# A decoder trunk: eight of the 22 row chunks of each down projection in seven products instead of eight

## The chip, the cores and the metric

One core of one Trainium2 chip runs the whole program. The metric is the device time in microseconds; several runs of each kernel are compared by their median.

## The reference

Two layers, each of three sublayers; x is 512 tokens by 1024 columns in float32, and the hidden width of the feed-forward is 2816.

```python
def swiglu_ffn(x, w_gu, w_down):
    a, u = jnp.split(x @ w_gu, 2, axis=-1)
    return (jax.nn.silu(a) * u) @ w_down

for l in range(DEPTH):                       # DEPTH = 2
    x = layer_norm(ALPHA * x + 0.5 * swiglu_ffn(x, ffn1_w_gu[l], ffn1_w_down[l]), ...)
    x = layer_norm(ALPHA * x + hybrid_mixer(x, w_in[l], w_out[l], ...), ...)
    x = layer_norm(ALPHA * x + 0.5 * swiglu_ffn(x, ffn2_w_gu[l], ffn2_w_down[l]), ...)
```

So there are four feed-forwards. Their down projection, h (512 x 2816) times w_down (2816 x 1024), is what the change concerns.

## The kernel before

**Three passes.** Every large product is made from operands cut in two float32r parts: `split` (L158) casts the high part on ScalarE (L159) and subtracts it from the source on VectorE (L160). `mm3` (L165) then multiplies high by high, high by low, low by high, three matmuls into one PSUM bank (L168, L169, L170).

**Weights.** `Weights` walks one list of items for the whole program. An item names a raw tile of 1 MB (two buffers, loaded on the queue of SyncE), and how to cut a *unit* from it: high and low part, each 128 x 1024, six buffers (`UBUFS`). `pump` cuts units up to `LOOK` = 6 ahead of their use; `done` gives buffers back and pumps. An item whose raw is None loads nothing.

**A feed-forward** (`ffn`, L434) has a gate/up stage and a down stage. The gate/up stage takes 11 pairs of 128 hidden rows. Nine of them (`SEVEN`) are already made in the seven-product form (`glu7`): `seven_items` (L276) forms sums of weight blocks on VectorE in tiles S (two buffers), and `sums_of_x` those of x in Th and Tl. The hidden values go to `hT`, 128 x 22 x 512. Before the last pair, the activations of the first two chunks are split ahead into a unit taken from the weights' pool (`early`, L568).

**The down stage** (L582) has all eight PSUM banks as `acc[t][q]`: four tiles of 128 tokens by two halves of 512 columns. For each of the first 18 chunks of 128 hidden rows it splits a chunk of `hT` two chunks ahead (`halves`; pool buffers hh and hl, four each), takes a weight unit of 128 rows x 1024 columns, and does `mm3` for each t and q: 24 matmuls of 128 x 128 by 128 x 512. The last four chunks (`TAIL`) are held in buffers of their own and done tile by tile, so that `norm` (L404) of a tile can run beside the next tile's matmuls. `norm` adds ALPHA times Y, the residual kept in SBUF, to the banks (L411), and does the layer norm on VectorE with one power on GpSimd (L419). Its scale and shift are loaded in chunk 7 (`load_ln`, L400).

**Order.** A framework sets the order of each engine's instructions when the program is built, by program order among those it holds to be ready, and places the semaphores. Tiles of one tag share their buffers in turn.

Of the kernel before, what the change touches and what calls it, by code (L numbers as in the profile page):

```python
# [7 lines left out]
F32 = mybir.dt.float32  # L8
F32R = mybir.dt.float32r
AF = mybir.ActivationFunctionType  # L10
ALU = mybir.AluOpType
# [17 lines left out]
TAIL = 4  # L29
# [3 lines left out]
DELAY = (4, 3, 9, 9)  # L33
# [59 lines left out]
class Trunk:  # L93
# [182 lines left out]
    def seven_items(self, a, u):  # L276


        sums = {}

        def blocks(v):
            h = KC // 2
            return v[:, :h, :P], v[:, h:, :P], v[:, :h, P:], v[:, h:, P:]

        def wide(t):
            return t.rearrange("p (k c) -> p k c", k=KC)

        def first(v, hi, lo):
            hv, lv = wide(hi), wide(lo)
            self.split(hv, lv, v[:, :, :P])  # L290
            return hv, lv

        def s12(q):
            def go(v, hi, lo):
                s = sums[q] = self.gpool.tile([P, 4, KC // 2, P], F32, tag="S", name=self.nm("S"), bufs=2)
                a11, a12, a21, a22 = blocks(v)
                self.nc.vector.tensor_add(s[:, 0], a21, a22)
# [25 lines left out]

    def ffn_items(self, gu, down, key):
        items = []
        for fp in range(NFP):
            a = self.cols_item(gu, fp * 256, (key, "a", fp))
            u = self.cols_item(gu, DFF + fp * 256, (key, "u", fp))
            if fp == 0:
                items += [a[0], u[0], a[1], u[1]]  # L330
            else:
                items += self.seven_items(a, u) if fp in SEVEN else a + u
        for fp in range(NFP):
            late = [self.tail_units if fp * 2 + c >= NF - TAIL else None for c in range(2)]
            items += self.rows_item(down, fp * 256, (key, "d", fp), late)
        return items

    def mix_items(self, w_in, w_out, key):
        items = self.cols_item(w_in, KA, (key, "kv"))
# [55 lines left out]
        self.to_xT(self.Y[:, t, 512:], t, 4)  # L395
        yield 0

    def load_ln(self, pool, g, b, tag="ln"):
        gb = pool.tile([P, 2, D], F32, tag=tag, name=self.nm("ln"))
        self.nc.sync.dma_start(gb[:, 0, :], g.partition_broadcast(P))  # L400
        self.nc.sync.dma_start(gb[:, 1, :], b.partition_broadcast(P))
        return gb[:, 0, :], gb[:, 1, :]

    def norm(self, t, halves, gb, out=None, delay=4):  # L404
        nc = self.nc
        g, b = gb
        y = self.Y[:, t, :]
        st = self.small.tile([P, 2, 6], F32, tag="st", name=self.nm("st"))
        for h in range(2):
            hs = slice(h * 512, (h + 1) * 512)  # L410
            nc.vector.scalar_tensor_tensor(out=y[:, hs], in0=y[:, hs], scalar=ALPHA, in1=halves[h],  # L411
                                           op0=ALU.mult, op1=ALU.add)
# [4 lines left out]
        nc.vector.tensor_scalar_add(ve, mv[:, 1:2], LN_EPS)  # L417
        rs = self.small.tile([P, 1], F32, tag="rs", name=self.nm("rs"))
        nc.gpsimd.tensor_tensor(out=rs, in0=ve, in1=self.mhalf[:, 0:1], op=ALU.pow)  # L419
# [11 lines left out]
    def tail_units(self):  # L431
        return self.units(self.fpool, "tl", TAIL)

    def ffn(self, g, b, out=None):  # L434
        nc, tc, W = self.nc, self.tc, self.W
        with ExitStack() as ctx:
            hpool = ctx.enter_context(tc.tile_pool(name=self.nm("ffnh"), bufs=1))
            gctx = ExitStack()
            gp = self.gpool = gctx.enter_context(tc.tile_pool(name=self.nm("ffng"), bufs=1))
            hT = hpool.tile([P, NF, SEQ], F32, name=self.nm("hT"))  # L440
# [94 lines left out]
            for fp in range(NFP):  # L535
                if fp == 0:
# [4 lines left out]
                    more = []  # L541
# [13 lines left out]
                if fp == 1:  # L555
                    a1, u0 = us[5], W.get()
                    for i in range(2):
                        t0 = i * 256
                        u = self.ps()
# [6 lines left out]
                    continue  # L566
                if fp == NFP - 1:
                    early = W.take()  # L568
                    hv = [v.rearrange("p (f t) -> p f t", f=2) for v in early]
                    self.split(hv[0], hv[1], hT[:, 0:2, :])  # L570
                if fp in SEVEN:
                    self.finish([xs])
                    glu7(fp)
# [12 lines left out]
            def halves():  # L586
                for f in range(2):
                    yield hv[0][:, f, :], hv[1][:, f, :]
                for f in range(2, NF):
                    hh = pool.tile([P, 512], F32R, tag="hh", name=self.nm("hh"), bufs=TAIL)  # L590
                    hl = pool.tile([P, 512], F32R, tag="hl", name=self.nm("hl"), bufs=TAIL)
                    self.split(hh, hl, hT[:, f, :])
                    yield hh, hl

            def down(f, u, h, t, q):
                ts = slice(t * P, (t + 1) * P)
                hs = slice(q * 512, (q + 1) * 512)
                self.mm3(acc[t][q], (h[0][:, ts], h[1][:, ts]), (u[0][:, hs], u[1][:, hs]), f == 0, f == NF - 1)

            split = halves()  # L600
            ahead = [next(split), next(split)]
            for f in range(NF - TAIL):
                if f == NF // 3:
                    gb = self.load_ln(pool, g, b)
                u, h = W.get(), ahead.pop(0)
                ahead.append(next(split))
                for t in range(NT):
                    for q in range(2):
                        down(f, u, h, t, q)
                    if t % 2:  # L610
                        self.step()
                W.done(2 if f == 1 else 1)
# [396 lines left out]
```

## Time and profile before

| | |
|---|---|
| median of 3 runs | 1847.43 us (1847.25 to 1847.91) |
| the profiled execution | 1847.67 us |
| its span in the profile | 1845.9 us |
| TensorE matmuls | 1831.1 us busy, 12170 instructions |
| VectorE | 1262.3 us busy |
| ScalarE | 841.9 us busy |
| GpSimd | 84.9 us busy |
| DMA | 184.89 MB, mean 100 GB/s |

PE is TensorE, PEld its weight loads, DVE is VectorE, ACT ScalarE, POOL GpSimd, SP SyncE; SPq is the queue from which SyncE issues transfers. A row of a group reads: line, engine, operation, output <- inputs, shapes, count | busy us, mean ns of one | idle us of the engine before them, and what ended it. A row of the order in time reads: start us, us, engine, line, operation, names, shapes, count [idle before, and what ended it]. A row of transfers reads: output <- input, queue, count, size of one, median us from issue to landing. A busy PE is not PE at its peak, since matmuls overlap.

### The profile page before, as it was taken

The numbers are of one execution on the slowest core, as the hardware profiler recorded it, in microseconds if no ns is written. First come the engines' busy times: TensorE is split into PE (matmuls) and PEld (weight loads), VectorE is DVE, ScalarE is ACT, GpSimd is POOL, SyncE is SP. The second block draws the span as 40 slices with busy tenths as digits, with TensorE's granted clock in tenths as the row PEclk, the third lists the DMA queues.
The fourth block names the chain that finished last, engine by engine and source line by source line (L and its number), as shares of the span: only waits on it lengthen the run. The fifth ranks groups of instructions, "written<-read, shape, count | busy, mean of one in ns | idle before, by whom it ended". The sixth has DMA issues, their size and how long they took to land.

```text
span 1845.9 us, 29148 instructions
## 1 busy us (share of the span) xinstructions
PE 1831.1 (99%) x12170; PEld 1669.2 (90%) x12170; DVE 1262.3 (68%) x1830; ACT 841.9 (46%) x1391; POOL 84.9 (5%) x72
## 2 busy tenths in 40 slices
PE   9999999999999999999999999999999999999998
PEld 9999988897789999988899999888877899999886
DVE  7788744656758788853687887447567687887435
ACT  4455533178723455543234555332786234555330
POOL 0000000111110000000000000001111100000001
PEclk9999999999999999999999999999999999999999
DMA  5233244122122322333312323341233122342321
GB/s 183 92 115 114 92 143 152 63 83 88 50 92 69 115 92 92 125 135 121 100 61 97 95 92 115 137 143 58 81 92 92 46 92 92 97 133 92 137 92 46
DMA packets 136948, 184.89 MB, mean 100 GB/s; under 512 B 3952, under 2 KB 115312, under 8 KB 136816
## 3 DMA queue, kind: packets, MB, share of 16 engines
q1 hardware_dynamic: 136816, 183.03, 30.4%
q8 instruction: 95, 1.56, 0.4%
q14 instruction: 37, 0.30, 0.1%
HBM read 180.92 MB, written 2.10 MB: 99 GB/s over the span
## 4 chain that ended last, share of the span: by engine, by line
PE 87%; issue 6%; DVE 3%; ACT 2%; DMA 1%; POOL 1%; SPq 0%; POOLq 0%; DVEq 0%; ACTq 0%
PE ps L168 28%; PE ps L169 28%; PE ps L170 28%; PE ps L388 1%; POOL sw L780 1%; DMA raw<-in_ffn_w_gu_dram 1%; ACT sw L778 1%; PE ps L888 0%; ACT b L820 0%; DMA retS<-c_retS_dram 0%; ACT uh L159 0%; DVE rr L853 0%; DVE Y L423 0%; DVE b L160 0%; PE ps L884 0%
## 5 line engine op out<-in xcount | busy, mean ns | idle before, releaser
L168 PE MATMUL ps<-xh,uh 128*128 128x256 f32 (+1 forms) x1616 | 482.8, 299 | 0.5 <-ACT uh L159 0.5
L169 PE MATMUL ps<-xl,uh 128*128 128x256 f32 (+1 forms) x1616 | 479.9, 297 | 0.3 <-DVE xl L160 0.3
L170 PE MATMUL ps<-xh,ul 128*128 128x256 f32 (+1 forms) x1616 | 479.7, 297 | 0.4 <-DVE ul L160 0.2
L160 DVE TENSOR_TENSOR ul<-raw,uh 128x1024 fp32r<-128x1024 f32 (+1 forms) x333 | 346.6, 1054 | 112.6 <-ACT uh L159 112.2
L159 ACT CAST uh<-raw 128x1024 fp32r<-128x1024 f32 (+1 forms) x333 | 299.1, 915 | 256.1 <-PE ps L169 172.3
L168 PE MATMUL ps<-Th,uh 128*128 128x256 f32 x1152 | 326.0, 283 | 0.0
L169 PE MATMUL ps<-Tl,uh 128*128 128x256 f32 x1152 | 326.0, 283 | 0.0
L170 PE MATMUL ps<-Th,ul 128*128 128x256 f32 x1152 | 326.0, 283 | 0.0
L168 PEld LDWEIGHTS ps<-xh,uh 128*128 128x128 f32 x1616 | 309.3, 191 | 10.8 <-issue 1.6
L170 PEld LDWEIGHTS ps<-xh,ul 128*128 128x128 f32 x1616 | 309.1, 191 | 9.2 <-DVE ul L160 0.8
L169 PEld LDWEIGHTS ps<-xl,uh 128*128 128x128 f32 x1616 | 309.3, 191 | 8.4 <-DVE xl L160 0.8
L168 PE MATMUL ps<-uh,hh 128*128 128x512 f32 x640 | 249.5, 390 | 0.0
L170 PE MATMUL ps<-uh,hl 128*128 128x512 f32 x640 | 249.0, 389 | 0.0
L169 PE MATMUL ps<-ul,hh 128*128 128x512 f32 x640 | 249.0, 389 | 0.0
L160 DVE TENSOR_TENSOR ul<-S,uh 128x1024 fp32r<-128x1024 f32 x144 | 175.9, 1222 | 73.5 <-ACT uh L159 72.9
L159 ACT CAST uh<-S 128x1024 fp32r<-128x1024 f32 x144 | 151.0, 1048 | 160.5 <-PE ps L169 159.2
L168 PEld LDWEIGHTS ps<-Th,uh 128*128 128x128 f32 x1152 | 221.2, 192 | 0.0
L169 PEld LDWEIGHTS ps<-Tl,uh 128*128 128x128 f32 x1152 | 221.2, 192 | 0.0
L170 PEld LDWEIGHTS ps<-Th,ul 128*128 128x128 f32 x1152 | 221.2, 192 | 0.0
L160 DVE TENSOR_TENSOR hl<-hT,hh 128x512 fp32r<-128x512 f32 x80 | 54.2, 690 | 173.4 <-ACT hh L159 173.4
L159 ACT CAST hh<-hT 128x512 fp32r<-128x512 f32 x80 | 48.6, 622 | 207.4 <-PE ps L169 206.2
L170 PEld LDWEIGHTS ps<-uh,hl 128*128 128x128 f32 x640 | 120.1, 188 | 25.0
(131 smaller groups left out, 2256.0 us busy)
## 6 DMA issues: line engine op xcount, KB each, us to landing
raw<-in_ffn_w_gu_dram SPq DMA_DIRECT2D x86, 1024.0 KB, 5.4
raw<-in_ffn_w_down_dram SPq DMA_DIRECT2D x44, 1024.0 KB, 4.9
raw<-in_w_in_dram SPq DMA_DIRECT2D x18, 1024.0 KB, 5.3
raw<-in_w_in_dram SPq DMA_DIRECT2D x8, 512.0 KB, 4.7
raw<-in_w_out_dram SPq DMA_DIRECT2D x8, 512.0 KB, 6.5
raw<-in_w_out_dram SPq DMA_DIRECT2D x4, 1024.0 KB, 4.9
ln<-in_ln_g_dram SPq DMA_DIRECT2D x6, 512.0 KB, 5.2
ln<-in_ln_b_dram SPq DMA_DIRECT2D x6, 512.0 KB, 6.5
```

The lines of the kernel that those rows point to most:

```text
L159: a = self.nc.scalar.copy(hi, src)
L160: b = self.nc.vector.tensor_sub(lo, src, hi.bitcast(F32))
L168: mm(out, ah, bh, start=start, stop=False, **kw)
L169: mm(out, ah, bl, start=False, stop=False, **kw)
L170: mm(out, al, bh, start=False, stop=stop, **kw)
L388: nc.tensor.transpose(b[:, c * P : (c + 1) * P], src[:, c * P : (c + 1) * P], self.ident)
L778: nc.scalar.copy(sw[q * 32 : q * 32 + 32, :n], src[o * 32 : o * 32 + 32, :n])
L780: nc.gpsimd.tensor_mul(sw[:, :n], sw[:, :n], S)
```

## The change

The first eight chunks, 1024 hidden rows, are taken as a product of 2 x 2 blocks: the activations in blocks of 256 tokens by 512 hidden rows, the weights in blocks of 512 hidden rows by 512 columns. Seven products of blocks take the place of eight. Each product has two steps (g = 0, 1) of 256 hidden rows, and a step has 12 matmuls on one weight unit (256 rows x 512 columns) and one activation pair.

- Weights: W11, W21 and W22 come as raw tiles (`wide_item`). Sums of blocks stand in two tiles R (tag S, now in a pool that lives as long as the feed-forward): W11 and W12 are loaded to them, and the other blocks are added by transfers with an adding operation, issued on GpSimd's queue. `cut` splits a unit from R and issues the next adds behind it.
- Activations: sums of blocks are formed in place in `hT` on VectorE (`fifth`, `third`).
- Products that belong to several blocks of the output are added up in the PSUM banks; where a bank holds a sum that another block needs, `into` puts it into Y with one VectorE operation, and the bank goes on.
- Chunk 8 stands between product 6 and product 7; chunks 9 to 21 are as before. `norm` scales Y by ALPHA only where `into` has not done so.
- The split ahead holds the operand of product 1 (256 tokens of four chunks). Scale and shift are loaded in chunk 12, in a buffer of R's tag.

```diff
-        for fp in range(NFP):
+        for fp in range(4, NFP):
...
+        return items + self.down_items(down, key, R, rows[0]) + rows[1:]
+
+    def down_items(self, w, key, R, row):
+        def block(i, j, g):
+            r0 = i * 512 + g * 256
+            return w[r0 : r0 + 256, j * 512 : (j + 1) * 512].rearrange("(k p) c -> p k c", p=P)
+        def add(g, x, i, j):
+            self.nc.gpsimd.dma_start(R[g][:, x], block(i, j, g), accum_op=ALU.add)
+        def begin(go):
+            def f(v, hi, lo):
+                for g in range(2):
+                    R[g] = self.spool.tile([P, 2, 2, 512], F32, tag="S", name=self.nm("R"), bufs=2)
+                    for x in range(2):
+                        self.nc.sync.dma_start(R[g][:, x], block(0, x, g))
+                    add(g, 0, 0, 1)
+                return go(v, hi, lo)
+            return f
+        def cut(g, x, *after):
+            def go(v, hi, lo):
+                hv, lv = (t.rearrange("p (k c) -> p k c", k=2) for t in (hi, lo))
+                self.split(hv, lv, R[g][:, x])
+                for a in after:
+                    add(g, *a)
+                return hv, lv
+            return (None, None, None, go)
+        p1, p2, p3 = (self.wide_item(w, j * 512, i, (key, "b", i, j)) for i, j in ((0, 0), (1, 0), (1, 1)))
+        p1[0] = p1[0][:3] + (begin(p1[0][3]),)
+        return (p1 + p2 + [cut(g, 0, (0, 1, 1), (1, 1, 1)) for g in range(2)]
+                + [cut(g, 0, (0, 1, 0)) for g in range(2)] + p3 + [cut(g, 1) for g in range(2)]
+                + [row] + [cut(g, 0) for g in range(2)])
...
+            def part(g, i, j):
+                return hT[:, j * 4 + 2 * g : j * 4 + 2 * g + 2, i * 256 : (i + 1) * 256]
+            def fifth(g):
+                a11, a21, a22 = part(g, 0, 0), part(g, 1, 0), part(g, 1, 1)
+                hh, hl = (v.rearrange("p (f t) -> p f t", f=2) for v in pair())
+                s1 = self.s1[:, g]
+                nc.vector.tensor_sub(s1, a21, a22)
+                nc.vector.tensor_sub(a21, a11, a21)
+                nc.vector.tensor_sub(a11, s1, a11)
+                self.split(hh, hl, s1)
+                return hh, hl
+            def third(g):
+                nc.vector.tensor_add(part(g, 0, 1), part(g, 0, 1), part(g, 0, 0))
+                return operand(part(g, 0, 1))
...
+            def seventh(banks, u, h, new):
+                for f in range(2):
+                    for i, b_ in enumerate(banks):
+                        ts = slice(i * P, (i + 1) * P)
+                        self.mm3(b_, (h[0][:, f, ts], h[1][:, f, ts]), (u[0][:, f, :], u[1][:, f, :]),
+                                 new and f == 0, False, skip_group_check=True)
+                self.step()
...
+            def into(banks, t0, q, scale, sign=ALU.add):
+                for i, b_ in enumerate(banks):
+                    y = self.Y[:, t0 + i, q * 512 : (q + 1) * 512]
+                    nc.vector.scalar_tensor_tensor(out=y, in0=y, scalar=scale, in1=b_, op0=ALU.mult, op1=sign)
+            for n, (banks, new, more) in enumerate((
+                    (low, True, (0, 0, ALPHA)), (left, True, None), (high, True, (0, 1, ALPHA)),
+                    (low, False, (0, 1, 1.0, ALU.subtract)), (right, True, None),
+                    (low, False, (2, 1, ALPHA, ALU.subtract)), (low, False, None))):
+                if n == 6:
+                    chunk(8)
+                for g in range(2):
+                    u, h = W.get(), ahead.pop(0)
+                    ahead.append(next(split))
+                    seventh(banks, u, h, new and g == 0)
+                    W.done(2 if n == 0 and g == 1 else 1)
+                if more:
+                    into(banks, *more)
+            for f in range(9, NF - TAIL):
+                if f == 12:
+                    gb = self.load_ln(self.spool, g_, b, "S", 2)
+                chunk(f)
...
-                self.norm(t, acc[t], gb, out, DELAY[t])
+                self.norm(t, acc[t], gb, out, DELAY[t], (1.0 if t < 2 else ALPHA, 1.0))
```

Here `low` and `high` are the banks of tokens 256 to 511, columns 0 to 511 and 512 to 1023, and `left` and `right` those of tokens 0 to 255. `ahead` holds activation pairs three steps ahead of their use, and `chunk` does the 24 matmuls of a chunk as before, the two banks of `low` last.

More of the change, by code (lines that the diff above doesn't have):

```diff
@@ L294, in go @@
             def go(v, hi, lo):
-                s = sums[q] = self.gpool.tile([P, 4, KC // 2, P], F32, tag="S", name=self.nm("S"), bufs=2)
+                s = sums[q] = self.spool.tile([P, 4, KC // 2, P], F32, tag="S", name=self.nm("S"), bufs=2)
                 a11, a12, a21, a22 = blocks(v)
@@ L402, in load_ln, with norm @@
         return gb[:, 0, :], gb[:, 1, :]
-    def norm(self, t, halves, gb, out=None, delay=4):
+    def norm(self, t, halves, gb, out=None, delay=4, scale=(ALPHA, ALPHA)):
         nc = self.nc
@@ L432, in tail_units, with ffn @@
         return self.units(self.fpool, "tl", TAIL)
-    def ffn(self, g, b, out=None):
+    def ffn(self, g_, b, out=None):
         nc, tc, W = self.nc, self.tc, self.W
@@ L584, in ffn, with pair @@
             acc = [[self.ps() for _ in range(2)] for _ in range(NT)]
-            def halves():
-                for f in range(2):
[L588 to L593, printed above, removed]
+            def pair():
+                return [pool.tile([P, 512], F32R, tag=tag, name=self.nm(tag), bufs=TAIL) for tag in ("hh", "hl")]
@@ new lines, in part, with operand @@
+            def part(g, i, j):
+                return hT[:, j * 4 + 2 * g : j * 4 + 2 * g + 2, i * 256 : (i + 1) * 256]
+            def operand(src):
+                hh, hl = (v.rearrange("p (f t) -> p f t", f=2) for v in pair())
+                self.split(hh, hl, src)
+                return hh, hl
+            self.s1 = pool.tile([P, 2, 2, 256], F32, tag="tlh", name=self.nm("s1"), bufs=TAIL)
+            def fifth(g):
+                a11, a21, a22 = part(g, 0, 0), part(g, 1, 0), part(g, 1, 1)
+                hh, hl = (v.rearrange("p (f t) -> p f t", f=2) for v in pair())
+                s1 = self.s1[:, g]
[3 more added lines that the diff above has]
+                self.split(hh, hl, s1)
+                return hh, hl
@@ new lines, in third, with whole, operands @@
+            def third(g):
+                nc.vector.tensor_add(part(g, 0, 1), part(g, 0, 1), part(g, 0, 0))
+                return operand(part(g, 0, 1))
+            def whole(f):
+                hh, hl = pair()
+                self.split(hh, hl, hT[:, f, :])
+                return hh, hl
+            def operands():
+                for g in range(2):
+                    yield operand(part(g, 0, 1))
+                for g in range(2):
+                    yield fifth(g)
+                for g in range(2):
+                    yield operand(part(g, 0, 0))
+                for g in range(2):
+                    yield third(g)
+                for g in range(2):
+                    yield operand(part(g, 1, 0))
+                yield whole(8)
+                for g in range(2):
+                    yield operand(part(g, 1, 1))
+                for f in range(9, NF):
+                    yield whole(f)
@@ L597, in down @@
                 hs = slice(q * 512, (q + 1) * 512)
[L598 to L604, printed above, removed]
+                self.mm3(acc[t][q], (h[0][:, ts], h[1][:, ts]), (u[0][:, hs], u[1][:, hs]), False, f == NF - 1,
+                         skip_group_check=True)
@@ L605, in ffn, with chunk @@
+            split = operands()
+            ahead = [(hv[0][:, g], hv[1][:, g]) for g in range(2)] + [next(split)]
+            def chunk(f):
                 u, h = W.get(), ahead.pop(0)
                 ahead.append(next(split))
[L607 to L610, printed above, removed]
+                for i, (t, q) in enumerate(((0, 0), (0, 1), (1, 0), (1, 1), (2, 1), (3, 1), (2, 0), (3, 0))):
+                    down(f, u, h, t, q)
+                    if i % 4 == 3:
@@ new lines, in ffn @@
+            for n, (banks, new, more) in enumerate((
[4 more added lines that the diff above has]
+                    chunk(8)
+                for g in range(2):
+                    u, h = W.get(), ahead.pop(0)
[4 more added lines that the diff above has]
+                    into(banks, *more)
```

21 lines of the change are left out of this document (13 added, 8 removed).

## The prediction

> **What bounds the kernel now.** I read the page's busy time and chain first, then the busy time in stretches, then the groups by shape, then the order of work around one down projection.
>
> ```profile
> PE 1831.1 (99%) x12170; PEld 1669.2 (90%) x12170; DVE 1262.3 (68%) x1830; ACT 841.9 (46%) x1391; POOL 84.9 (5%) x72
> ...
> PE 87%; issue 6%; DVE 3%; ACT 2%; DMA 1%; POOL 1%; SPq 0%; POOLq 0%; DVEq 0%; ACTq 0%
> ```
>
> TensorE is busy 1831.1 of 1845.9 us and the chain lies on it for 87%. The stretches are the 18 chunks of the first down projection (its last four come behind them), some gate/up work, and the first 5.5 us of the same projection.
>
> ```profile
> core 0: us, PE busy (x) PEld busy (x) DVE busy (x) ACT busy (x) POOL busy (x), PEclk, DMA share, GB/s
> 239.00:337.10 98.10, 98.10 (x435) 81.26 (x434) 41.05 (x43) 33.96 (x43) 0.00 (x0) 1.00 0.43 140
> 571.50:670.00 98.50, 98.50 (x768) 96.02 (x767) 84.41 (x116) 44.44 (x65) 3.04 (x2) 1.00 0.34 108
> 239.00:244.50 5.50, 5.50 (x27) 4.54 (x26) 4.06 (x6) 3.13 (x5) 0.00 (x0) 1.00 0.90 309
> ```
>
> In the down projection TensorE has no gap and the granted clock is 1.00, while VectorE works 41.05 of 98.10 us. So a matmul taken out there is worth its whole spacing, as long as what replaces it stays under the cover. The gate/up row shows how far cover reaches: VectorE busy 84.41 of 98.50 us and TensorE still without a gap.
>
> ```profile
> L168 PE MATMUL ps<-uh,hh 128*128 128x512 f32 x640 | 249.5, 390 | 0.0
> L168 PE MATMUL ps<-uh,uh 128*128 128x512 f32 x64 | 24.9, 390 | 0.0
> ```
>
> The order in time, TensorE and then VectorE:
>
> ```profile
> 238.89 0.28 PE L170 MATMUL ps<-Th,ul 128*128 128x256 f32 x1
> 239.01 0.40 PE L168 MATMUL ps<-uh,uh 128*128 128x512 f32 x1
> ...
> 294.06 0.69 DVE L160 TENSOR_TENSOR hl<-hT,hh 128x512 fp32r<-128x512 f32 x1 [3.27 <-ACT hh L159]
> ...
> 337.58 0.69 DVE L160 TENSOR_TENSOR hl<-hT,hh 128x512 fp32r<-128x512 f32 x1 [3.27 <-ACT hh L159]
> ```
>
> The two groups before are one of the three passes of all down matmuls: 704 over four projections, 176 each, 8 for each of 22 chunks. Their 390 ns overlap, so the price is the spacing: the activation split comes once a chunk, and from 294.06 to 337.58 lie 8 chunks, 5.44 us each, 24 matmuls of 226.7 ns.
>
> **The change: matmuls.** Eight chunks cost 8 x 24 = 192 matmuls. The form with seven products costs 7 x 2 steps x 12 = 168, with the same operand shapes. Per projection 24 go, 5.44 us; over four, 96, 21.76 us. A step of 12 takes 2.72 us; I count time T from the projection's first matmul (239.01), so step k starts at 2.72 k, products 1 to 6 fill steps 0 to 11, chunk 8 runs from 32.6 to 38.1, and product 7 follows.
>
> [...]
>
> **The change: VectorE and ScalarE.** Prices from the groups, then the order in time at the start of a projection:
>
> ```profile
> L160 DVE TENSOR_TENSOR ul<-raw,uh 128x1024 fp32r<-128x1024 f32 x227 | 276.2, 1221 | 95.7 <-ACT uh L159 95.4
> L159 ACT CAST uh<-raw 128x1024 fp32r<-128x1024 f32 x227 | 237.0, 1049 | 190.6 <-PE ps L169 110.9 <-DMA raw<-in_ffn_w_gu_dram 32.7 <-PE ps L170 20.9
> L160 DVE TENSOR_TENSOR hl<-hT,hh 128x512 fp32r<-128x512 f32 x80 | 54.2, 690 | 173.4 <-ACT hh L159 173.4
> L159 ACT CAST hh<-hT 128x512 fp32r<-128x512 f32 x80 | 48.6, 622 | 207.4 <-PE ps L169 206.2 <-DVE ul L160 1.3
> L297 DVE TENSOR_TENSOR S<-raw 128x512 f32<-128x512 f32 x72 | 49.5, 688 | 1.4 <-DMA raw<-in_ffn_w_gu_dram 0.3
> L411 DVE SCALAR_TENSOR_TENSOR Y<-Y,ps 128x512 f32<-128x512 f32 x48 | 32.7, 683 | 25.8 <-PE ps L170 25.4
> ```
>
> ```profile
> 239.28 0.42 DVE L521 SCALAR_TENSOR_TENSOR hT<-ps,s 128x256 f32<-128x256 f32 x1 [0.59 <-PE ps L170]
> 240.17 1.23 DVE L160 TENSOR_TENSOR ul<-raw,uh 128x1024 fp32r<-128x1024 f32 x1 [0.46 <-ACT uh L159]
> 241.31 2.49 DVE L160 TENSOR_TENSOR hl<-hT,hh 128x512 fp32r<-128x512 f32 x4
> 250.97 2.36 DVE L160 TENSOR_TENSOR ul<-raw,uh 128x1024 fp32r<-128x1024 f32 x2 [3.99 <-ACT uh L159]
> 240.04 2.18 ACT L159 CAST hh<-hT 128x512 fp32r<-128x512 f32 x4
> 244.67 1.05 ACT L159 CAST uh<-raw 128x1024 fp32r<-128x1024 f32 x1 [2.45 <-PE ps L170]
> ```
>
> Per projection come six more weight splits (14 for 8), six more activation splits (14 for 8), six subtractions for product 3, two additions for product 5, and eight updates of Y from the banks (rows of L411's kind). VectorE: 6 x 1.22 + 6 x 0.69 + 8 x 0.69 + 8 x 0.68 = 22.4 us. ScalarE: 6 x 1.05 + 6 x 0.62 = 10.0 us. ScalarE needs 1.67 us in a step of 2.72 and is no limit.
>
> VectorE is tight. Its strictest date is the start of product 6 (step 10, T = 27.2), which needs the update of Y after product 4 because it adds into the same banks. Due by then, from T = 0.7 when the gate work's last piece (239.28) ends: 7 weight splits, 9 activation splits, 8 sums, 6 updates. At single durations 8.5 + 6.2 + 5.5 + 4.1 = 24.3 of 26.5 us; at the rates of the runs of four and two (0.62 and 1.18 us apart) 22.5. Laying the pieces one behind another, each no earlier than its buffer is free, I get no TensorE wait at the second rate and 1.67 us at the first (in steps 9 and 10). Four projections: 0 to 6.7 us. The queued work of this kernel shows the second rate, so I take a sixth, 1.1 us.
>
> Each update of Y waits for TensorE to end its product; behind it on VectorE stand later splits. The order is not the program's: the casts of four activation chunks run at 240.04, ahead of the weight cast that the program has second and that runs at 244.67. So a piece that is known to wait lets ready ones pass. Within the other dates: the first activation split that is not done ahead (product 2, T = 5.4) ended at about 242, T = 3; the split done ahead covers only product 1, 5.4 us where it was 10.9.
>
> **The change: loads, adds, queues.**
>
> ```profile
> q1 hardware_dynamic: 136816, 183.03, 30.4%
> raw<-in_ffn_w_down_dram SPq DMA_DIRECT2D x44, 1024.0 KB, 4.9
> raw<-in_w_in_dram SPq DMA_DIRECT2D x8, 512.0 KB, 4.7
> raw<-in_ffn_w_gu_dram SPq DMA_DIRECT2D x3, 512.0 KB, 7.6
> ```
>
> ```profile
> 225.82 1.23 DVE L160 TENSOR_TENSOR ul<-S,uh 128x1024 fp32r<-128x1024 f32 x1 [0.52 <-ACT uh L159]
> 232.78 6.30 SPq L265 DMA_DIRECT2D raw<-in_ffn_w_down_dram  x2
> 239.73 0.34 SPq L400 DMA_DIRECT2D ln<-in_ln_g_dram  x1
> 240.12 0.42 SPq L401 DMA_DIRECT2D ln<-in_ln_b_dram  x1
> 344.53 1.52 POOL L419 TENSOR_TENSOR rs<-ve,mhalf 128x1 f32<-128x1 f32 x1 [343.23 <-DVE ve L417]
> ```
>
> SP loses one load of 1 MB per projection (10 for 11) and gets four of 512 KB into the sum tiles. They wait for the last reading of the gate work's S tiles (225.82 to 227.05, T = -12); what stands behind them, the load at 232.78, comes later than four issues of 0.4 us, so nothing is held. At 309 GB/s the 2 MB are in by about T = -4; a first add to each half follows, due before the split at T = 0 and at the latest 2.3 us before step 4, T = 8.6. Two adds of 3.1 us meet both. The scale and shift loads move from chunk 7 to 12; they land within 8 us and are due 30 us later. Both cost nothing; their cover is the six units of lookahead.
>
> POOL issues eight adds of 512 KB per projection; it has no other work there (idle 343.23 us until 344.53). No row shows an adding transfer. Lower end: the plain load, 1.5 us of all engines (0.90 share gave 309 GB/s) and 4.7 us to landing. An add has twice to read, so 3.1 us apart and 7.6 us to landing is my middle; the upper end is one after another at 7.6 us each. The binding chain: the split of product 3's weights (steps 4, 5) reads the sums, then POOL adds two blocks for each half, and product 4's second half (step 7, T = 19.0) needs its split, 2.3 us, so the third add must have landed by 16.8. First adds are released at about 2.4, the third at 5.9. Middle: max(5.9, 2.4 + 6.2) + 7.6 = 16.2, no wait. At the plain end it lands at 10.6. At c us each in series it lands at 2.4 + 3c: a wait beyond c = 4.8, and 8.4 us per projection at 7.6. I take 0, since with the transfers at 43% share in this stretch adds overlap as plain loads do. None of it can be a gain: TensorE has no gap here that could close.
>
> **Sum.** The profiled execution took 1847.67 us, 0.24 over the median of 1847.43. 1847.67 - 21.76 + 1.1 = 1827.0.
>
> **Rivals.**
> - VectorE is the bound in the products, or adds of 4.8 to 6.3 us in series hold product 4. For it: only 2 us are spare at T = 27.2. Against: the gate/up row with VectorE at 84.41 of 98.50 and no gap. Time: 1832.6 with VectorE's whole 6.7 us; up to 1843.9 with the adds at 6.3 us (4.5 us each projection).
> - Slower: the adds run in series at more than 6.9 us each. The wait lies before step 6 or 7 of each projection; it eats 5.44 us at c = 6.6 and more beyond. At c = 7.6, 1847.67 - 21.76 + 33.6 = 1859.5. For it: nothing in the trace bounds an add from above. Against: a plain 512 KB needs 1.5 us of the engines.
>  [...]
> - No change: c near 6.6 us, gain and wait equal, 1847.7.
>
> **How the numbers follow.** Full gain 0.63 (1824.5 to 1830), part of it held back 0.20 (1830 to 1843.9), no change 0.04, slower 0.13. About 0.2% (3.7 us) is what a measurement of this kernel can tell from no change. Faster is 0.63 + 0.20 = 0.83. The low end is 1825.9 less 1.4 for run and clock differences; the range to 1841 takes in the full gain and most of the second case and leaves out about 0.2.
>
> **What would show it.** Right: one pass of the down matmuls counts 672 for 704; each projection starts and ends 5.44 us nearer; VectorE at 1262 + 90, ScalarE at 842 + 40; TensorE without a gap in the first 44 us of a projection; adds landing under 8 us. Wrong: rows of matmuls of the products that waited on the split of the sum tile, whose cast waited for a transfer (the adds), or on a split whose VectorE piece began late (the crowd), or on an update of Y; or a spacing in the products that isn't 226.7 ns.

## The result and the profile after

The changed kernel takes 1903.28 us (1901.65 to 1903.95), the kernel before, beside it, 1847.53 us: a ratio of 1.030, 95% interval 1.0282 to 1.0318. The forecast was 1827.0 us. One run of one later kernel, the one with six sums on VectorE, took 2981.46 us at a granted clock of 0.555, against 0.999 in its other three, and is left out below.

The page of the changed kernel, its busy times, the engines' shares of the chain and the group of the adds:

```profile
PE 1823.9 (96%) x12074; PEld 1657.7 (87%) x12074; DVE 1341.5 (71%) x1942; ACT 879.6 (46%) x1439; POOL 124.3 (7%) x104
...
PE 77%; issue 10%; DVE 5%; DMA 3%; ACT 2%; POOL 2%; SPq 0%; POOLq 0%; DVEq 0%; ACTq 0%
...
R<-in_ffn_w_down_dram POOLq DMA_DIRECT2D x32, 512.0 KB, 6.0
```

TensorE has 96 matmuls fewer (12074 for 12170), as the change says. Its share fell from 99% to 96%: in a span of 1902.2 us it is not busy for 78.3 us, where it was 14.8. The adds land in 6.0 us, under the 7.6 that the forecast took for one add. So a single add is no slower than thought. The waits show what is wrong:

```profile
PE ps L168 <- ACT hh L159: 56.4, 4, 14.3
PE ps L170 <- DVE hl L160: 5.5, 8, 1.3
```

One long wait in each of the four projections, on the cast of an *activation*, an operand that needs no add. In the first projection (its first matmul starts at 239.45), TensorE's waits and then ScalarE's order in time:

```profile
252.30 0.50 PE L170 MATMUL ps<-uh,hl 128*128 128x512 f32 x1 [1.33 <-DVE hl L160]
269.14 0.80 PE L168 MATMUL ps<-uh,hh 128*128 128x512 f32 x1 [14.29 <-ACT hh L159]
```

```profile
239.53 1.05 ACT L159 CAST uh<-R 128x1024 fp32r<-128x1024 f32 x1 [0.93 <-PE ps L169]
...
248.74 1.05 ACT L159 CAST uh<-R 128x1024 fp32r<-128x1024 f32 x1 [6.59 <-DMA R<-in_ffn_w_down_dram]
261.26 1.04 ACT L159 CAST uh<-R 128x1024 fp32r<-128x1024 f32 x1 [11.48 <-DMA R<-in_ffn_w_down_dram]
267.53 1.04 ACT L159 CAST uh<-R 128x1024 fp32r<-128x1024 f32 x1 [5.22 <-DMA R<-in_ffn_w_down_dram]
268.48 0.61 ACT L159 CAST hh<-s 128x512 fp32r<-128x512 f32 x1
```

The four casts from R are the weights of product 3 (steps 4 and 5) and product 4 (steps 6 and 7). The last three waited for adds. The cast of 268.48 is the activation of step 5; it came behind both weight casts of product 4, before which ScalarE stood idle for 11.48 and 5.22 us. VectorE has the same order. The second row is the difference that this cast reads, the first the weight split of product 4 ahead of it:

```profile
262.34 1.22 DVE L160 TENSOR_TENSOR ul<-R,uh 128x1024 fp32r<-128x1024 f32 x1 [9.50 <-ACT uh L159]
...
264.08 0.68 DVE L645 TENSOR_TENSOR s<-hT 128x512 f32<-128x512 f32 x1
```

So an operand that needs no add was held on two engines by splits that wait for adds. Ahead of ScalarE's last weight cast, and with VectorE's order as it is, it could have come at 264.8, some 3.7 us earlier (an estimate from these rows). GpSimd's adds in the same projection:

```profile
226.13 1.35 POOL L349 DMA_DIRECT2D R<-in_ffn_w_down_dram  x1 [224.82 <-DVE Q L530]
232.47 1.23 POOL L349 DMA_DIRECT2D R<-in_ffn_w_down_dram  x1 [4.99 <-issue]
242.62 1.21 POOL L349 DMA_DIRECT2D R<-in_ffn_w_down_dram  x1 [8.91 <-DVE hl L160]
248.98 1.23 POOL L349 DMA_DIRECT2D R<-in_ffn_w_down_dram  x1 [5.15 <-issue]
255.22 1.21 POOL L349 DMA_DIRECT2D R<-in_ffn_w_down_dram  x1 [5.01 <-issue]
261.50 1.22 POOL L349 DMA_DIRECT2D R<-in_ffn_w_down_dram  x1 [5.07 <-DMA R<-in_ffn_w_down_dram]
267.77 1.21 POOL L349 DMA_DIRECT2D R<-in_ffn_w_down_dram  x1 [5.04 <-DMA R<-in_ffn_w_down_dram]
273.66 1.22 POOL L349 DMA_DIRECT2D R<-in_ffn_w_down_dram  x1 [4.68 <-DVE hl L160]
```

Six of them follow the one before at 5.9 to 6.4 us, about when that one has landed. The third comes 10.15 us behind the second, which took 9.9 us to land, beside a plain load of 1 MB issued at 233.22. In the order of the built program the second and the fourth of them are W22 for product 6, which has until T = 27. The adds that product 4 needs come fifth (255.22) and sixth (261.50). The sixth is landed at 267.5, and the cast starts at 267.53.

The last part is the clock. A table by stretch, the column behind POOL being the granted clock:

```profile
255.00:260.00 5.00, 0.00 (x0) 0.00 (x0) 0.00 (x0) 0.00 (x0) 1.21 (x1) 0.95 0.62 92
260.00:265.00 5.00, 0.00 (x0) 0.00 (x0) 2.66 (x4) 1.04 (x1) 1.22 (x1) 0.50 0.34 45
265.00:270.00 5.00, 0.85 (x2) 0.50 (x2) 1.76 (x3) 2.47 (x4) 1.21 (x1) 0.50 0.47 79
270.00:275.00 5.00, 4.28 (x10) 3.14 (x10) 5.00 (x7) 3.59 (x6) 1.22 (x1) 0.50 0.59 98
275.00:280.00 5.00, 5.00 (x20) 3.98 (x19) 4.87 (x7) 2.03 (x3) 0.00 (x0) 0.85 0.88 198
```

During the wait the clock falls to 0.50 and stays there for some 7 us after the matmuls go on. So a wait is paid twice.

### The profile page after: what moved, and what is told of

Same layout as the page of the kernel before. It is cut to its first block, busy times and chain, and to the rows that moved or that the text cites. A ratio compares the mean times of both kernels' runs of the same rounds, so it can differ in the third digit from the quotient of the medians.

```text
span 1902.2 us, 29290 instructions
## 1 busy us (share of the span) xinstructions
PE 1823.9 (96%) x12074; PEld 1657.7 (87%) x12074; DVE 1341.5 (71%) x1942; ACT 879.6 (46%) x1439; POOL 124.3 (7%) x104
## 3 DMA queue, kind: packets, MB, share of 16 engines
q1 hardware_dynamic: 143152, 187.23, 30.4%
## 4 chain that ended last, share of the span: by engine, by line
PE 77%; issue 10%; DVE 5%; DMA 3%; ACT 2%; POOL 2%; SPq 0%; POOLq 0%; DVEq 0%; ACTq 0%
PE ps L170 25%; PE ps L169 25%; PE ps L168 25%; DMA R<-in_ffn_w_down_dram 1%; ACT sw L896 1%; POOL sw L898 1%; DMA raw<-in_ffn_w_gu_dram 1%; POOL R L349 1%; PE ps L426 1%; DVE Y L462 1%; DVE st L452 1%; DVE ul L160 1%; ACT uh L159 1%; DVE Y L459 1%; DVE Y L450 0%
## 5 line engine op out<-in xcount | busy, mean ns | idle before, releaser
L159 ACT CAST uh<-raw 128x1024 fp32r<-128x1024 f32 (+1 forms) x325 | 291.1, 912 | 229.7 <-PE ps L169 149.3
L160 DVE TENSOR_TENSOR ul<-raw,uh 128x1024 fp32r<-128x1024 f32 (+1 forms) x325 | 336.7, 1049 | 83.5 <-ACT uh L159 83.0
L168 PE MATMUL ps<-uh,hh 128*128 128x512 f32 x640 | 254.5, 398 | 56.4 <-ACT hh L159 56.4
L170 PE MATMUL ps<-uh,hl 128*128 128x512 f32 x640 | 254.1, 397 | 5.5 <-DVE hl L160 5.5
L169 PE MATMUL ps<-ul,hh 128*128 128x512 f32 x640 | 253.1, 395 | 0.0
L168 PEld LDWEIGHTS ps<-uh,hh 128*128 128x128 f32 x640 | 122.9, 192 | 83.3 <-ACT hh L159 58.1
L169 PEld LDWEIGHTS ps<-ul,hh 128*128 128x128 f32 x640 | 122.7, 192 | 25.6
```

Source lines behind the costliest of these rows:

```text
L159: a = self.nc.scalar.copy(hi, src)
L160: b = self.nc.vector.tensor_sub(lo, src, hi.bitcast(F32))
L168: mm(out, ah, bh, start=start, stop=False, **kw)
L169: mm(out, ah, bl, start=False, stop=False, **kw)
L170: mm(out, al, bh, start=False, stop=stop, **kw)
```

## The experiments

Theory A, after this reading: only one add is under way at a time, since the room that the program reserves for GpSimd's transfers (`dynamic_dma_scratch_size`) holds no second one. With the runs it grew: the order on GpSimd, ScalarE and VectorE, and the clock behind a wait, came to it. What it and its rivals mean for a run is said in each expectation. Ratios are against the kernel before, in runs on the same chip.

**Room for two adds.** The program sets this room, here 1024 bytes.

```diff
-    nc = _bacc.Bacc("TRN2", target_bir_lowering=False, num_devices=1, dynamic_dma_scratch_size=1024)
+    nc = _bacc.Bacc("TRN2", target_bir_lowering=False, num_devices=1, dynamic_dma_scratch_size=1920)
```

> Only the space reserved per partition for the descriptors of GpSimd's transfers grows, from 1024 to 1920 bytes. Theory A (the space holds one add of 512 KB, so that an add is issued only when the one before has landed, 6.2 us apart): adds overlap, are issued about 1.2 us apart where nothing else holds them and land about 3.3 us apart; TensorE's wait of 14.3 us in each projection goes; time 1826 to 1832. Theory B (GpSimd or its queue takes one adding transfer at a time whatever the space): adds stay 6.2 us apart, time 1900 to 1906. Theory C (VectorE is the bound in the products and the adds matter little): some waits stay, on late VectorE pieces, time 1833 to 1890.

Measured: 1856.14 us, ratio 1.0047 (1.003 to 1.0064). 47 of the 56 us are gone, but the number expected was missed. GpSimd's adds, and TensorE's waits:

```profile
225.31 1.35 POOL L349 DMA_DIRECT2D R<-in_ffn_w_down_dram  x1 [224.00 <-DVE Q L530]
227.40 1.21 POOL L349 DMA_DIRECT2D R<-in_ffn_w_down_dram  x1 [0.74 <-DMA R<-in_ffn_w_down_dram]
...
241.51 1.21 POOL L349 DMA_DIRECT2D R<-in_ffn_w_down_dram  x1 [4.23 <-DVE ul L160]
246.02 1.20 POOL L349 DMA_DIRECT2D R<-in_ffn_w_down_dram  x1 [3.30 <-DVE ul L160]
```

```profile
PE ps L168 <- ACT hh L159: 11.9, 4, 3.2
PE ps L170 <- DVE hl L160: 5.2, 4, 1.5
```

The second add now starts 2.1 us behind the first, and product 4's adds at 241.51 and 246.02, not 255.22 and 261.50. They wait for VectorE's split, as the program wants. What is left is 17.1 us of listed waits, all on the activation of step 5, 11.9 of them on its cast, and TensorE busy for 1821.6 us where 1808.8 would do (below). In the first projection ScalarE's cast (254.89) now follows close on the difference that it reads; that one VectorE formed only at 254.17, behind the weight split of 252.43, whose cast waited for an add. So the room is one cause and not the only one. The time lies in theory C's range too; the run without adds (below) speaks against C, since VectorE has the same work there and no wait in the products.

**The same bytes in smaller adds.** Room as in the changed kernel, each add as two of 256 KB.

```diff
-            self.nc.gpsimd.dma_start(R[g][:, x], block(i, j, g), accum_op=ALU.add)
+            for k in range(2):
+                self.nc.gpsimd.dma_start(R[g][:, x, k], block(i, j, g)[:, k], accum_op=ALU.add)
```

> Each add of 512 KB is issued as two of 256 KB, in the space of 1024 bytes. Theory A: two or three of the small adds are in flight at a time, so an add's two halves together take less than 6.2 us, and the time falls below 1880. Theory B: each half is waited for by itself, about 3 us of fixed time and 1.6 us of transfer, 9 us for an add; time above 1930.

Measured: 1861.72 us in a single run, below 1880, as theory A has it. The halves overlap: three of them start within 2.85 us from 225.90, and a half lands 5.7 us after issue in the median. So in this run neither the queue nor the adding operation kept transfers apart. At 1024 bytes three halves were thus under way together, and the fourth started at 230.30; at 1920 bytes a second whole add started 2.1 us behind the first (above).

**The order of the adds alone.** Those for product 6 are tied behind those for products 3 and 4 and, as the pairs in the edit stand, each also behind product 7's add of its half; room as in the changed kernel.

```diff
+            if self.adds:
+                self.tc.add_manual_dep(a.ins, self.adds[-1].ins.name, NOSYNC, reason="add order")
...
-        return (p1 + p2 + [cut(g, 0, (0, 1, 1), (1, 1, 1)) for g in range(2)]
-                + [cut(g, 0, (0, 1, 0)) for g in range(2)] + p3 + [cut(g, 1) for g in range(2)]
+        return (p1 + p2 + [cut(g, 0, (0, 1, 1)) for g in range(2)]
+                + [cut(g, 0, (0, 1, 0), (1, 1, 1)) for g in range(2)] + p3 + [cut(g, 1) for g in range(2)]
```

> The two adds for product 6 in each projection, which the order of the changed kernel puts second and fourth on GpSimd's queue, go behind the adds for product 4 and later; nothing else changes, and adds stay one at a time. Theory A: the third add of the queue, which product 4 waits for, is issued at about T = 3.5 where it was the fifth at T = 16; product 4's weights are split 10 us earlier; what is left is about 4 us a projection for the activation cast that stands behind the last of these casts on ScalarE; time 1840 to 1855. Theory B the same. Theory C (VectorE): the wait shrinks by less than half, time above 1870.

Measured: 1931.39 us, ratio 1.0456 (1.044 to 1.0471). Worse than the changed kernel, the opposite of what was expected. TensorE's waits in the first projection:

```profile
257.63 0.79 PE L168 MATMUL ps<-uh,hh 128*128 128x512 f32 x1 [5.15 <-ACT hh L159]
...
274.51 0.50 PE L170 MATMUL ps<-uh,hl 128*128 128x512 f32 x1 [3.78 <-DVE hl L160]
289.08 0.80 PE L168 MATMUL ps<-uh,hh 128*128 128x512 f32 x1 [10.81 <-ACT hh L159]
```

The first wait shrank from 14.29 to 5.15, but two new ones came behind it, at steps 8 and 9. These steps are product 5, whose activation pieces stand on VectorE behind the weight splits of product 6 (272.63 and 285.30), and product 6's casts start at 271.56 and 284.23, as its adds land, now the sixth and the eighth. Eight adds 6.25 us apart are 50 us, and the products last 43.5 us, but the first two adds were issued before the products began (225.29 and 233.27). In fifth and sixth place product 6's adds would have landed near 262 and 271 (an estimate from this run's landings), with product 7's behind them. That order was not run. So this run shows its own order to be worse, and not that no order of single adds would do.

**No adds at all.**

```diff
-            self.nc.gpsimd.dma_start(R[g][:, x], block(i, j, g), accum_op=ALU.add)
+            pass
```

> All adds are left out, so the weight sums of products 3, 4, 6 and 7 are not formed; matmuls, splits, loads and updates of Y stay. Theories A and B: TensorE has no gap in the products, time 1825 to 1829, the saving of the 96 matmuls in full. Theory C: waits on VectorE stay, 0.4 us to 1.7 us a projection or more, time 1828 to 1840.

Measured: 1825.85 us, ratio 0.9884 (0.987 to 0.9899). Its page, and a table of the first 11 us of the first projection:

```profile
PE 1808.8 (99%) x12074; PEld 1650.9 (91%) x12074; DVE 1339.3 (73%) x1942; ACT 881.1 (48%) x1439; POOL 84.8 (5%) x72
```

```profile
239.00:250.00 11.00, 11.00 (x50) 9.10 (x49) 11.00 (x14) 7.01 (x10) 0.00 (x0) 1.00 0.24 93
```

No wait in the products is left, with VectorE full for these 11 us and in each stretch up to 265. This is what the change is worth without its adds, 21.4 us under the kernel before in that comparison, and VectorE's crowd costs nothing measurable. It also separates the two prices of the wait: against this kernel the changed one has TensorE not busy for 63.3 us more (78.3 for 15.0), and busy for 15.1 us more with the same matmuls. The latter is the clock: 0.981 in the mean for 0.999, and 395 to 398 ns for one of these matmuls where it was 389 to 390.

**Room and order together.**

> Both edits together: room for 1920 bytes of descriptors, and the adds for product 6 put behind those for products 3 and 4. Left over after the room alone were 3.2 and 1.5 us of TensorE wait in a projection, and a granted clock of 0.61 to 0.71 for about 10 us behind them. Theory A (each add is late because of where it stands and of how many can be under way; a wait costs itself and a stretch of low clock): the two adds for product 4 start near 241 and land by 250 to 252, the weight casts and the activation behind them are in time to within 1.5 us; 1826 to 1838 us. Rival B (the order of the adds does nothing once they overlap; the activation cast stands behind the weight casts anyway): 1850 to 1858 us, with the same two waits.

Measured: 1876.45 us, ratio 1.0157 (1.0142 to 1.0172), against both. ScalarE and TensorE in the first projection:

```profile
268.19 1.04 ACT L159 CAST uh<-R 128x1024 fp32r<-128x1024 f32 x1 [8.37 <-DMA R<-in_ffn_w_down_dram]
```

```profile
253.90 0.50 PE L170 MATMUL ps<-uh,hl 128*128 128x512 f32 x1 [0.97 <-DVE hl L160]
273.05 0.79 PE L168 MATMUL ps<-uh,hh 128*128 128x512 f32 x1 [8.43 <-ACT hh L159]
```

Product 4 had no wait, and the activation of step 5 waited only 0.97 us. The long wait is at step 9, the second half of product 5: the sum for its activation stood on VectorE behind product 6's second weight split (269.27). The cast of that split is the one of 268.19. It waited for the last add, issued at 256.14, which took 12.0 us to land, beside a plain load of 1 MB issued at 257.35. Here too product 7's adds stand ahead of product 6's. So last is too late for product 6's adds; whether the early place that they have in the changed kernel is the best one, this run does not show.

**Room, and the activation ahead.** The operands of product 3 are cut before product 1.

```diff
-            ahead = [(hv[0][:, g], hv[1][:, g]) for g in range(2)] + [next(split)]
+            ahead = [(hv[0][:, g], hv[1][:, g]) for g in range(2)] + [next(split) for _ in range(4)]
...
-                    ahead.append(next(split))
+                    if 2 * n + g > 2:
+                        ahead.append(next(split))
```

> Room for 1920 bytes of descriptors, adds in the order of the changed kernel, but the operands of product 3 are cut ahead of product 1, so that on ScalarE they stand before the weight casts of product 4 that wait for adds. Theory A (the wait at step 5 is a cast that was ready and stood behind two casts that were not): the waits of 3.2 and 1.5 us go, the granted clock stays at 1.00, 1826 to 1834 us. Rival B (the weights of product 4 come too late themselves): the wait moves to step 6 or 7 with 2 us or more, the clock falls again, 1845 to 1858 us.

Measured: 1846.20 us, ratio 0.9994 (0.9985 to 1.0004): between the two expectations. ScalarE in the first projection:

```profile
251.09 1.06 ACT L159 CAST uh<-R 128x1024 fp32r<-128x1024 f32 x1 [7.05 <-DMA R<-in_ffn_w_down_dram]
252.04 0.61 ACT L159 CAST hh<-s 128x512 fp32r<-128x512 f32 x1
```

The program now has the activation first, and the scheduler still put it (its source was formed at 244.6) behind a weight cast that waited 7.05 us for its add. The waits are now many and small, the longest 1.0 us, and the granted clock stays at 1.00 in every stretch from 239 to 300.

Tied in front of that cast:

```diff
+                if (0, 1, 0) in after:
+                    self.tc.add_manual_dep(self.p_cast.ins, self.p_before[0].ins.name, NOSYNC, reason="order")
```

> As the kernel with more room and early operands for product 3, and besides the activation cast of product 3's second half is tied to stand before the weight cast of product 4 on ScalarE (the scheduler had put it behind again, at 252.04 after the weight cast of 251.09, which waited 7.05 us for its add). Theory C (what is left there is VectorE's backlog: it stood idle 6.35 of 26.5 us behind that cast, with about 2 us to spare): the cast is early, but VectorE still stands idle near 5 us for the add, small waits on activation splits remain: 1834 to 1844 us. Rival A2 (the misplaced cast was the whole of it): no wait, 1826 to 1830 us.

Measured: 1838.83 us, ratio 0.9955 (0.994 to 0.997), as theory C has it. The cast's place was worth some 7 us; small waits on activation splits remain (12, the longest 1.0 us). The weight cast still waits for its add, and VectorE works 2.79 us of the stretch from 250 to 255, to be full from 255 to 270.

**Sums on an engine.** In the next kernels W12 comes from the other half of the sum tile, and W22 from the stage of product 5. First on GpSimd, with only the two last adds as transfers:

```diff
-                    add(g, 0, 0, 1)
+                    self.nc.gpsimd.tensor_add(R[g][:, 0], R[g][:, 0], R[g][:, 1])
...
+                self.nc.gpsimd.tensor_add(R[g][:, 0], R[g][:, 0], w22)
+                self.split(hv, lv, R[g][:, 0])
+                self.nc.gpsimd.tensor_add(R[g][:, 1], R[g][:, 1], w22)
+                add(g, 0, 1, 0)
```

> Six of the eight adds of a projection are no transfers any more: GpSimd adds tiles that lie in SBUF already (W12 in the other half of the sum tile, W22 in the stage from which product 5 is cut). Two adds (the last ones) stay transfers. Room for descriptors as in the changed kernel. Theory A: with any sum of under 4.8 us on GpSimd product 4 is in time, no TensorE wait, clock 1.00, 1826 to 1830 us. Rival B (GpSimd's sums are slower than 4.8 us each, or slow VectorE down beside them): waits before step 6 as in the changed kernel, above 1847 us.

Measured: 1864.30 us, ratio 1.0092 (1.0077 to 1.0107). A sum takes 2.4 to 3.1 us, in the range that theory A allowed, and yet it is slower. GpSimd and then VectorE:

```profile
238.69 6.29 POOL L376 TENSOR_TENSOR R<-R,raw 128x1024 f32<-128x1024 f32 x2 [2.93 <-DMA raw<-in_ffn_w_down_dram]
```

```profile
240.47 2.24 DVE L656 TENSOR_TENSOR s<-hT 128x512 f32<-128x512 f32 x1
242.64 3.42 DVE L160 TENSOR_TENSOR ul<-R,uh 128x1024 fp32r<-128x1024 f32 x1
...
249.39 0.68 DVE L657 TENSOR_TENSOR hT<-hT 128x512 f32<-128x512 f32 x1
250.00 1.21 DVE L160 TENSOR_TENSOR ul<-R,uh 128x1024 fp32r<-128x1024 f32 x1
```

Beside GpSimd's sums a VectorE piece of 0.68 us takes 2.24 and one of 1.21 takes 3.42. Over the program VectorE is busy for 1377.0 us, against 1339.3 with as many instructions in the run without adds. So rival B was right in its second half: GpSimd's sums slow VectorE down.

The same six sums on VectorE (`vector` for `gpsimd` in the diff above; the first of them stands directly ahead of its split):

> As the kernel before it, but the six sums are on VectorE: 6 x 1.22 = 7.3 us more VectorE work in a projection, due by T = 27. Theory A with the prediction's count of VectorE (24.3 of 26.5 us taken): 31.6 us do not fit, a wait of up to 5 us in a projection and a dip of the clock: 1835 to 1855 us. Rival B (VectorE had more room than counted, as the run without adds hints): 1826 to 1831 us.

Measured: 1835.65 us, ratio 0.9936 (0.9919 to 0.9952), the low end of theory A. One wait in a projection is left, and the granted clock stays at 1.00. With the operands of product 3 ahead and tied:

> The kernel with its six sums on VectorE (1835.7, one TensorE wait of 1.71 us in a projection, on the activation cast of product 3's second half at 253.62), with that operand cut ahead of product 1 and the sums for product 4 tied behind it. Theory A (that cast's place is the wait): no wait, 1826 to 1829 us. Rival D (VectorE is full: 31.6 us of work for 26.5): the wait moves to step 6 or to the splits behind it, 1832 to 1842 us.

Measured: 1834.66 us, ratio 0.9937 (0.9921 to 0.9954). The waits, before and with that order:

```profile
PE ps L168 <- ACT hh L159: 6.8, 4, 1.7
```

```profile
PE ps L171 <- DVE hl L160: 3.2, 4, 0.8
```

The wait moved to a split and the time stayed, as rival D has it: VectorE, with 7.3 us more to do, is full in each stretch from 239 to 270. The next run takes part of that work away.

**Four sums on VectorE, four adds by transfer.** As the kernel before, but the two sums for product 6 are transfers again, with room for one add.

```diff
-                self.nc.vector.tensor_add(R[g][:, 1], R[g][:, 1], w22)
+                add(g, 1, 1, 1)
```

> As the kernel before it, but the two sums for product 6, which have time until T = 27, are transfers again: four adds of a projection by transfer, none of them due within 16 us of its issue, four sums on VectorE (4.9 us in place of 7.3). Room for descriptors as in the changed kernel (one add under way at a time). Theory A: adds cost nothing where two of them fit before their date, no wait, 1826 to 1829 us. Rival D (VectorE full at 29.2 us of 26.5): a small wait, 1829 to 1836 us. Rival E (any add by transfer beside the products slows TensorE or its feeding): above 1836 us.

Measured: 1827.28 us, ratio 0.9896 (0.9882 to 0.9911). This beats both kernels. GpSimd's adds, and the row of the first 11 us again:

```profile
228.60 1.36 POOL L350 DMA_DIRECT2D R<-in_ffn_w_down_dram  x1 [227.29 <-ACT Q L558]
235.07 1.23 POOL L350 DMA_DIRECT2D R<-in_ffn_w_down_dram  x1 [5.11 <-DVE Q L566]
251.52 1.21 POOL L350 DMA_DIRECT2D R<-in_ffn_w_down_dram  x1 [15.22 <-DVE ul L160]
257.66 1.23 POOL L350 DMA_DIRECT2D R<-in_ffn_w_down_dram  x1 [4.93 <-issue]
```

```profile
239.00:250.00 11.00, 11.00 (x50) 9.12 (x49) 11.00 (x16) 5.72 (x10) 0.00 (x0) 1.00 0.36 117
```

Two pairs, 6.5 and 6.1 us apart, one at a time as before, and nobody waits: each add has 16 us or more until its date. TensorE has no wait in the first projection's products. So four adds by transfer in a projection did not disturb TensorE, busy for 61.00 of the 61.00 us from 239 to 300 (rival E falls); what counted in these runs is when they land.

The same without the early operands and the tie:

> As the kernel with four sums on VectorE and four adds by transfer, but without the early operands of product 3 and without the tie on ScalarE: the order of ScalarE's casts is the scheduler's. It tells whether that order costs something by itself once the sums are in time. Theory A (the place of the cast in the queue matters only behind a weight cast that waits for an add): within 0.2% of the kernel with both, 1826 to 1830 us, or at most one wait of 1 to 2 us in a projection as in the kernel with six sums on VectorE (1.71 us there, on the same cast), up to 1836 us. Rival F (the order is as heavy as the adds): above 1840 us.

Measured: 1830.64 us, ratio 0.9911 (0.9895 to 0.9928). The intervals of the last two overlap. Waits on that cast make 1.5 us in all, the longest 1.1. Whether the order is worth something here stays open; it is little.

## Why the prediction was wrong

**The matmuls: right.** 96 fewer, forecast 21.76 us; without the adds the kernel is 21.4 us faster. That is 223 ns for each of them, so the runs bear out the 226.7 ns of the trace before.

**VectorE and ScalarE: right in kind, small in size.** Forecast 90 and 40 us more; VectorE has 79.2 more (1341.5 for 1262.3), ScalarE 37.7 (879.6 for 841.9). Of the 1.1 us for the crowd nothing was measurable. The limit that the count pointed at is real: four sums more in a projection are still hidden, six are not (1827.3 and 1834.7 us). In the first projection two of them run 11 and 6 us ahead of the products (226.7 and 232.0 with four sums), so four sums add 2.4 us to the 24.3 that the prediction counted against 26.5.

**The adds: the step that failed.** "I take 0, since with the transfers at 43% share in this stretch adds overlap as plain loads do." They did not overlap. The argument looked at the share of the transfer engines, which is not what kept them apart: it was the room (with more of it the second add started 2.1 us behind the first), which no row of the trace before could show, since no such transfer was in it. One add took less than forecast (6.0 for 7.6 us to landing), but the next started 6.25 us later and not 3.1.

That alone, put into the prediction's formula, gives 2.4 + 3 x 6.25 = 21.2 against 16.8, a wait of 4.4 us in a projection and 1844.4 us, at the upper end of the prediction's "part of it held back". Three more steps failed. The first three sizes below are worked out from the rows of the first projection, the fourth is measured; none of the first three was taken away by itself without touching another.

- *The order of the adds.* The formula has three adds in series from T = 2.4 on, the last of them for product 4's second half. In the run they are four, the third to the sixth, from T = 3.2 on, since the adds for product 6 stand second and fourth and one for product 3 between them. The sixth landed at T = 28.1 (267.5), with its split done near T = 30.4, for a step due at 19.0. That is 11.3 us late where 4.4 was worked out: 7 us more.
- *"So a piece that is known to wait lets ready ones pass."* On ScalarE it did not. The order is set when the program is built, and the program itself cuts weights up to six units ahead of their use and activations three steps ahead. So on ScalarE both weight casts of product 4 come before the cast of step 5's activation, and on VectorE the first of their splits comes before its difference. An activation that needed no add stood behind two splits that did, and the wait came at step 5, not 7. In the first projection the waits up to 271.09 (1.33, 14.29 and 0.72 us) make 16.3 us, 5 more than 11.3.
- *The clock.* The sum has no term for it. It costs 15.1 us, 3.8 in a projection.

4.4 + 7 + 5 + 3.8 = 20.2 us in a projection; measured are 77.4 / 4 = 19.4 (1903.28 less 1825.85). The rival "slower" had the right cause (adds in series), but put the wait before step 6 or 7, its point at 6.9 us each and its price at 1859.5; in this order 6.25 us is far past the point.

## What to carry to other kernels

A kind of transfer that the trace has not shown needs a bound on how many can be under way, not only on its duration; count adds times their distance against the date of each reader, and if they don't fit, form the sums on an engine that has room for them, and leave to transfers those with the latest dates. Idle time alone is not room: GpSimd's sums here slowed VectorE (2.24 us for a piece of 0.68). Where the order is static, ask what stands behind each instruction that could wait, on each engine: here an activation that needed no add, its difference on VectorE and its cast on ScalarE, paid for two weight splits that did. On this kernel matmuls also ran at about half the pace (0.43 us apart for 0.23) behind TensorE waits of 3.78 to 14.29 us, and at a granted clock of 0.50 behind smaller ones close together (3.19 and 1.51 us, 2.15 and 0.96 us), for 7.4 us behind the longest, so price such waits twice.

## What the runs showed of the hardware

**The clock falls behind a wait.** TensorE's matmuls around the end of the low stretch in the changed kernel:

```profile
275.52 0.63 PE L168 MATMUL ps<-uh,hh 128*128 128x512 f32 x1
275.94 0.63 PE L169 MATMUL ps<-ul,hh 128*128 128x512 f32 x1
276.37 0.47 PE L170 MATMUL ps<-uh,hl 128*128 128x512 f32 x1
276.69 0.40 PE L168 MATMUL ps<-uh,hh 128*128 128x512 f32 x1
```

The spacing is 0.43 us up to 276.4 and 0.23 from 276.7, 7.4 us after the matmuls went on. Gaps of 8.43 us (room and order together) and 3.78 us (the order of the adds alone) did the same, one of 1.71 us (six sums on VectorE) did not. Behind the gap of 3.78 us the spacing was 0.42 to 0.43 us from 275.94 until TensorE's next wait began at 278.27. It need not be one gap: with room for two adds the gaps were 3.19 and 1.51 us, and with GpSimd's sums 2.15 and 0.96 us with two matmuls between them, and in both the clock fell to 0.50. So among the single gaps here the clock fell at 3.78 us and not at 1.71, and in the last case gaps that are all shorter than 3.78 us were enough (one of 2.09 us ended 4.7 us before that of 2.15 did).

**An add by transfer.** 512 KB land 6.0 us after issue in the median of the changed kernel and 8.2 us with room for two; beside a plain load of 1 MB single ones took 9.9 and 12.0 us (above). While an add is moving alone, it fills the transfer engines:

```profile
q0 software_dynamic: 193, 0.36, 100.1%
```

That is a stretch of 2 us (246 to 248) of the changed kernel; the columns are packets, MB and the share of 16 engines' time. 0.36 MB in 2 us are 0.18 MB each us, about half the 0.34 of plain loads in the trace before (309 GB/s at a share of 0.90), so by estimate some 2.9 us of the 6.25 are transfer, and the rest passes before and behind it.
